# Value projections with tokens on partitions: 512 moving columns and four open PSUM banks in place of 256 columns and one

## The chip, the cores and the metric

The program runs on one core of a Trainium2 chip. The metric is device time in microseconds (us) of one execution, from the first to the last instruction; smaller is better. The kernel before has a median of 3309.61 us over three runs.

## The reference, cut to what matters

Two transformer blocks run one after the other on 512 tokens of 1024 channels, each with two layers. In the first block the normalised input h is multiplied by one wide matrix; the parts va and vb of the product are the values of two attention mixers:

```python
h = rmsnorm(x, norm1[l])
proj = h @ w_in[l]
qa, ka, va, qb, kb, vb, gate_pre = jnp.split(proj, splits, axis=-1)
o_a = dilated_mixture(hd4(qa, 12), hd4(ka, 12), hd4(va, 12))   # heads of 64, three groups of 4
o_b = stick_breaking_attention(hd4(qb, 4), hd4(kb, 4), hd4(vb, 4))
```

va has 768 columns (three head groups of 256), vb has 256. The second block does the same for two streams of tokens, 512 "latent" and 256 "context" tokens. Its mixer is a gated scan whose values are 512 columns of the input projection, plus a differential attention whose values are 256 columns, plus a Fourier part. Everything is float32; the kernel must come close to float32 results.

## The kernel before, in words

Activations lie with channels on partitions, as eight k tiles of 128 channels. To reach float32 accuracy each activation and each weight is kept as two parts, hi and lo, of a 32-bit format that TensorE multiplies in one pass, and each product is three matmuls: hi·hi, hi·lo, lo·hi.

Most projections (`proj_t`, with `mm3`, lines 131 to 142) take 128 weight columns as the stationary operand and 512 tokens as the moving one: 24 matmuls of 512 columns for one output tile. The value projections need tokens on partitions. `proj_n` (line 144) therefore takes 128 tokens of the activation as the stationary operand and 256 weight columns as the moving one: 24 matmuls of 256 columns for one block of 128 tokens, into one PSUM bank, of which they use half. Every matmul has its own weight load.

In the first block, `mixer1` (line 249) calls it for four chunks of 256 columns in each layer: vb right behind its queries and keys (lines 300 to 306); and behind the keys and queries of the other mixer three chunks, one for each head group of va (lines 313 to 320). The first of these takes blocks of 128 consecutive tokens. The other two take the tokens b, b + 4, b + 8, ...: the stationary operand is then read with a step of four elements,

```python
slice(b, T, 4) if c else slice(b * P, (b + 1) * P)
```

so 192 of the 384 value matmuls of a layer have stepped weight loads. Each block's result goes from PSUM to SBUF by one ScalarE instruction (line 306 or 320).

In the second block `natural` (line 760) does the same for the values of both streams (two chunks of 256 columns, called by `values`, line 858) and for the values of the differential attention (one chunk, called by `diff_in`, line 1159). Evacuations alternate between ScalarE (line 772) and VectorE (line 770). In the first layer the latent values stand behind the context's output projection and norm; in the second layer `weave` mixes them with the context's residual and norm steps, one step for each `yield`.

Weights come by `load_weights` (line 116) in pieces of 1024 columns on 128 partitions (512 KB): one DMA on SyncE's queue, a cast on ScalarE (hi, line 126), a subtraction on VectorE (lo, line 127). There are three buffers for raw, three for hi and two for lo. `weights` (line 106) gives the chunk that is wanted and asks for the next one; a chunk of 128 columns is one piece (all eight k tiles), a chunk of 256 columns is two pieces (four k tiles each).

PSUM in the mixer of the first block is cut into two "mm" banks, three "sc" banks for scores, two "at" and one "po"; in the second block's mixer into two "mm", two "lev", two "at" and a "ds" tile of two banks. Each engine works through its queue in order; the framework lays the queues out ahead of time, by the order of the program's text and by when operands are ready in its own planning.

Of the kernel before, what the change touches and what calls it, by code (L numbers as in the profile page):

```python
# [14 lines left out]
ALU = mybir.AluOpType  # L15
# [15 lines left out]
class Split:  # L31
    """A value kept as two float32r parts, each of [128, n]: hi + lo."""
# [8 lines left out]
class Stream:  # L41
    """Tokens that go through the second block: x tiles [128 channels, n]."""
# [5 lines left out]
class Net:  # L48
# [57 lines left out]
    def weights(self, src, kt, cols, ahead=True):  # L106
        """src: DRAM [128, kt, cols]; -> list over k of (hi, lo) slices. ahead: asks for the next ones, too."""
        self.asked.append((src.tensor.name, src.offset, [list(d) for d in src.ap], kt, cols))
        i = len(self.asked)
        out = self.ahead.pop() if self.ahead else self.load_weights(src, kt, cols)  # L110
        if ahead and i < len(self.plan):
            name, off, ap, kt, cols = self.plan[i]
            self.ahead.append(self.load_weights(bass.AP(self.io[name].tensor, off, ap), kt, cols))
        return out
# [22 lines left out]
    def proj_t(self, out, w, c0, xs, start=True, stop=True):  # L137
        """out[128 n, t] += W[:, c0:c0+128]^T x over the k tiles of xs."""
        for k, x in enumerate(xs):
            hi, lo = w[k]  # L140
            self.mm3(out, hi[:, c0:c0 + P], lo[:, c0:c0 + P], x.hi, x.lo,
                     start and k == 0, stop and k == len(xs) - 1)

    def proj_n(self, out, w, c0, n, xs, ts):
        """out[128 t, n] = x[:, ts]^T W[:, c0:c0+n]; ts: 128 tokens, a slice or the first one."""
# [9 lines left out]

    def split(self, dst, src, lo_src=None):
        """dst = src as two parts; src is float32 in SBUF or PSUM."""
# [14 lines left out]
    def rstd_cols(self, acc, nb, dim, classes=False):  # L172
        """acc [128, nb*128] of squares -> [128 t, nb] of 1/sqrt(mean + eps); column b is a block of tokens or,
        by classes, the tokens b, b + nb, ..."""
# [11 lines left out]
    def rstd_bcast(self, acc, nb, dim):  # L186
        """-> PSUM [128, nb*128]: 1/sqrt(mean + eps) of each token on every partition."""
# [14 lines left out]
    def gained(self, l, name, k):  # L202
        """x[k] * g as a split tile; the token's factor comes behind the product."""
# [7 lines left out]
    def token_factor(self, acc, classes=False):  # L211
        """1/rms of each token: on every partition, [128, t], and [128 t, block]; with classes also
        [128 i, r] of the tokens 4 i + r."""
# [7 lines left out]
    def scope(self, banks=None, **pools):  # L221
        """Opens pools for a part of the program; the exit stack closes them.
        banks: PSUM tag -> number of banks."""
# [25 lines left out]
    def mixer1(self, l, first):  # L249
# [24 lines left out]
        def proj_qk(c, n, scale):  # L274
            """-> [128 ch, t] tiles; those of the dilated groups, from the third of twelve heads' on, keep
            the tokens by classes: column 128 r + i is token 4 i + r."""
# [23 lines left out]
        w = self.weights(io["w_in_n"][l, 3], KT, 256)  # L300
        rh = self.small("rh", 4)
        nc.vector.tensor_scalar(rh, rcs[0], 0.5, None, ALU.mult)
        for b in range(4):
            ps = self.bank()
            self.proj_n(ps[:, :256], w, 0, 256, hs, b * P)
            nc.scalar.mul(vb[:, b, :], ps[:, :256], rh[:, b:b + 1])
        qa = proj_qk(0, 6, 0.125)
        ka = proj_qk(6, 6, 1.0)
# [4 lines left out]
        for i in range(3):  # L313
            w = self.weights(io["w_in_n"][l, i], KT, 256)
            c, j = min(i, 1), max(i - 1, 0)
            for b in range(4):
                ps = self.bank()
                self.proj_n(ps[:, :256], w, 0, 256, hs, slice(b, T, 4) if c else slice(b * P, (b + 1) * P))
                dst = va[c][b][:, 4 * j:4 * j + 4, 0:64]
                nc.scalar.mul(dst, ps[:, :256].rearrange("p (h d) -> p h d", h=4), rcs[c][:, b:b + 1])  # L320

        ob = [self.pv.tile([P, 256], F32, tag=f"ob{b}", name=self.nm("onat")) for b in range(4)]
        # sums of the dilated mixture by blocks (0) and classes (1) of tokens, with negated maxima and denominators
# [49 lines left out]
    def after(self, ins, before):  # L373
        """Keeps `ins` behind `before` in their engine's queue."""
# [58 lines left out]
    def weighted(self, out, blocks, width):  # L433
        """out[128 q, width] = sum over blocks of p^T-transposed @ v: blocks (p [128 q, 128 s], v [128 s, width])."""
# [14 lines left out]
    def dsw(self, s, qa, ka, va, sums, stat):  # L449
        """Head slot s of the three dilated groups: the first one's queries by blocks of 128 tokens, those of  # L450
        the other two, which see keys of their own class t % 4 alone, by classes and with one softmax."""
# [36 lines left out]
    def dsw_join(self, sums, stat):  # L488
        """The mixture over all three groups: sums times exp(max - joint max) / joint denominator. Each layout gets
        the other's maxima and denominators by way of memory. -> by layout, normalised [128 t, 256] tiles."""  # L490
# [27 lines left out]
    def stick(self, h, qb, kb, vb, on):  # L518
        """Head h of the stick-breaking mixer. With y = tanh(z / 2): sigmoid(z) = (1 + y) / 2 and
        1 - sigmoid(z) = (1 - y) / 2, whose product over the later keys is a scan from the right;  # L520
        the half of sigmoid is in vb."""
# [21 lines left out]
    def heads_t(self, on, name, classes=None):  # L543
        """[128 t, 256] of four blocks -> two split tiles [128 ch, t]; classes: a part to add, by classes."""
# [32 lines left out]
    def consts2(self):  # L577
# [12 lines left out]
        # forget gates f = mid + half * tanh(z / 2) and 1 - f = half - half * tanh(z / 2): [128, layer, dir * head]  # L590
# [19 lines left out]
    def lambdas(self):  # L610
        nc, io, pc = self.nc, self.io, self.pcx
        self.onorm, self.subln, self.neglam = [], [], []
        # the halves of the silus are in the values and in onorm
# [21 lines left out]
    def cond(self):  # L635
        """silu of both conditions, on every partition."""
# [11 lines left out]
    def modulation(self, l, before):  # L648
# [11 lines left out]
        for v in range(2):  # L660
            m = self.mods[l][v]
            nc.vector.tensor_tensor(m, m, self.v2("b_mod", 48 * l, 48), ALU.add)
            # 1 + scale times the norm's gain; gates times the gain behind them
# [10 lines left out]
    def adaln_steps(self, hs, st, m, sc, sh, alloc):  # L674
        """rms_norm(x) * gain * (1 + scale) + shift as split tiles."""
# [12 lines left out]
    def weave(self, first, *rest, rate=1.0):  # L688
        """Interleaves two chains of steps, rate of the second to one of the first; the second starts first."""
# [14 lines left out]
    def residual(self, st, acc, ys, m, gate, out=None, pe=False):  # L704
        """x += gate * rms_norm(y), in steps. out: the last one, which stores x. pe: TensorE sums the
        squares, for a norm that waits for them."""
# [25 lines left out]
    def pairs(self, pool, tag, name, n, bufs=None):  # L732
        """Allocator of split tiles of n tokens, packed into slots of 4 KB."""
# [26 lines left out]
    def natural(self, l, st, hs, first, out, scale=1.0):  # L760
        """Projection with tokens on partitions into the blocks out[b] [128, width]."""
        nc = self.nc
        for i in range(out[0].shape[1] // 256):
            w = self.weights(self.io["w_in2n"][l, first + i], KT, 256)
            for b, o in enumerate(out):
                ps = self.bank()
                self.proj_n(ps[:, :256], w, 0, 256, hs, b * P)
                dst = o[:, 256 * i:256 * (i + 1)]
                if b % 2:
                    nc.vector.tensor_scalar(dst, ps[:, :256], scale, None, ALU.mult)  # L770
                else:
                    nc.scalar.mul(dst, ps[:, :256], scale)
                yield

    def mixers2(self, l, st, sc, c, full):
        """Both streams' mixers. c: the context's input; full: the context goes on behind this layer.
        -> both streams' input of the feed forward."""
# [44 lines left out]
        else:  # L822
            # the second half's products lie behind the first half's norms; cat's tiles become the output
# [15 lines left out]
    def gpairs(self, name):  # L839
        """Allocator of the context's split tiles in the slots of the gates."""  # L840
# [17 lines left out]
    def values(self, l, st, hs, v):  # L858
        yield from self.natural(l, st, hs, 0, v, 0.5)

    def attend(self, l, st, hs, sc, v, side=iter(())):
        """The hgrn heads, the differential attention between their parts, the fourier input.
        side: steps that go along; the context's projections come first."""
# [32 lines left out]
    def mix_cat(self, l, st, a, alloc):  # L896
        """The mixer's output in front of the output projection."""
# [9 lines left out]
    def mix_out(self, l, st, cat, ys, acc, order=range(KT), kept=None):  # L907
        """The output projection of st's tokens, and its sum of squares. kept: weights by chunk, to which
        the last two are added."""
# [20 lines left out]
    def halves(self, st):  # L930
        """The stream's tokens in two parts, as (slice, stream)."""
# [10 lines left out]
    def gate(self, l, h, d, hs, n, t):  # L942
        """t = tanh(z / 2) of the forget gate, d: 0 forward, 1 backward."""
        self.nc.scalar.activation(t, self.proj2(l, 4 + 4 * d + h, hs, n), AF.Tanh, scale=0.5)

    def silu2(self, dst, ps, n):
        """2 * silu."""
# [4 lines left out]
    def state(self, st, h, kx, v):  # L952
        """Final states of the context: sum over tokens of key x value, keys kx [128 ch, (f, b), n]."""
# [14 lines left out]
    def states(self, l, st, h, hs, v):  # L968
        """The context's final states of a head, by products over the later or earlier gates."""
# [677 lines left out]
```

## Time and profile before

| | |
|---|---|
| runs, device time | 3307.6, 3309.61, 3320.05 us |
| median | 3309.61 us |
| profiled execution, span (the page has no other time of it) | 3308.6 us |
| TensorE matmul busy | 3250.8 us, 98% |
| TensorE weight loads busy | 2760.6 us, 83% |
| VectorE, ScalarE, GpSimd busy | 61%, 41%, 2% |
| DMA | 370.70 MB, mean 112 GB/s |
| mean granted TensorE clock | 0.993 of full speed |

A matmul's duration in the profile runs from its issue to its modelled end, so that neighbours overlap: matmuls of 512 columns start 0.23 us apart and last 0.39 us each. How fast TensorE goes is read from the starts (or from a count in a stretch), not from durations.

### The profile page before, as it was taken

The page shows a single profiled execution, that of the slowest core. Times are in us where ns is not written, and L with a number is a line of the kernel's source. Part 1 is how long each engine was busy: PE and PEld are TensorE (multiplying, and loading weights), DVE is VectorE, ACT ScalarE, POOL GpSimd, SP SyncE. Part 2 cuts the span into 40 slices and gives each one's busy share as a digit, 9 for nine tenths or more (in the row PEclk, how much of TensorE's full clock was granted, in tenths as well). Part 3 has the DMA queues.
Part 4 walks back from the last instruction along what each step waited for, and adds up shares of the span by engine and source line. Part 5 has one row for each costly group of instructions (what it writes and reads, how often), then busy time and mean ns, then how long its engine had stood idle before and what let it go on. Part 6 is the DMA issues. An engine that isn't in the chain of part 4 may idle for free. (4 is left out here: it accounts for less than half of the span.)

```text
span 3308.6 us, 48142 instructions
## 1 busy us (share of the span) xinstructions
PE 3250.8 (98%) x19480; PEld 2760.6 (83%) x19480; DVE 2006.8 (61%) x3318; ACT 1358.9 (41%) x2326; POOL 68.6 (2%) x213
## 2 busy tenths in 40 slices
PE   9999999999999999999999999999999999999998
PEld 7978888888978888889887789888899988888887
DVE  4265799753255799766867867333257677662335
ACT  3144432332144432346756755222235457542223
POOL 0000000000000000000100000000000100000000
PEclk9999999999999999999999999999999999999999
DMA  4213367533213366536342225333134522223333
GB/s 139 70 45 98 114 197 216 151 98 96 71 45 97 109 199 216 151 102 189 106 140 64 73 68 166 96 96 96 59 94 147 165 83 70 68 86 96 96 96 115
DMA packets 109231, 370.70 MB, mean 112 GB/s; under 512 B 13264, under 2 KB 18384, under 8 KB 109008
## 3 DMA queue, kind: packets, MB, share of 16 engines
q1 hardware_dynamic: 103824, 352.28, 35.0%
q0 software_dynamic: 5184, 15.34, 1.6%
q8 instruction: 153, 2.51, 0.3%
q14 instruction: 70, 0.57, 0.1%
HBM read 359.64 MB, written 7.93 MB: 111 GB/s over the span
## 5 line engine op out<-in xcount | busy, mean ns | idle before, releaser
L126 ACT CAST whi<-raw 128x1024 fp32r<-128x1024 f32 (+1 forms) x556 | 575.9, 1036 | 1137.9 <-PE mm L134 785.8
L127 DVE TENSOR_TENSOR wlo<-raw,whi 128x1024 fp32r<-128x1024 f32 (+1 forms) x556 | 667.0, 1200 | 383.8 <-PE mm L135 171.8
L133 PE MATMUL mm<-h,whi 128*128 128x512 f32 x1904 | 752.1, 395 | 11.9 <-ACT whi L126 6.7
L135 PE MATMUL mm<-h,wlo 128*128 128x512 f32 x1904 | 752.0, 395 | 0.0
L134 PE MATMUL mm<-h,whi 128*128 128x512 f32 x1904 | 750.5, 394 | 0.0
L133 PEld LDWEIGHTS mm<-h,whi 128*128 128x128 f32 x1904 | 358.4, 188 | 85.3 <-issue 8.4
L135 PEld LDWEIGHTS mm<-h,wlo 128*128 128x128 f32 x1904 | 358.1, 188 | 73.0 <-DVE wlo L127 1.7
L134 PEld LDWEIGHTS mm<-h,whi 128*128 128x128 f32 x1904 | 358.2, 188 | 72.7 <-issue 1.5
L135 PE MATMUL mm<-hid,wlo 128*128 128x512 f32 (+1 forms) x896 | 323.8, 362 | 3.2 <-DVE wlo L127 3.1
L133 PE MATMUL mm<-hid,whi 128*128 128x512 f32 (+1 forms) x896 | 324.1, 362 | 0.4 <-ACT whi L126 0.4
L134 PE MATMUL mm<-hid,whi 128*128 128x512 f32 (+1 forms) x896 | 324.3, 362 | 0.0
L135 PEld LDWEIGHTS mm<-hid,wlo 128*128 128x128 f32 x896 | 168.0, 188 | 31.4 <-DVE wlo L127 3.8
L134 PEld LDWEIGHTS mm<-hid,whi 128*128 128x128 f32 x896 | 168.2, 188 | 28.1 <-DVE hid L160 0.4
L133 PEld LDWEIGHTS mm<-hid,whi 128*128 128x128 f32 x896 | 168.1, 188 | 28.1 <-ACT whi L126 0.6
L133 PE MATMUL mm<-cat,whi 128*128 128x512 f32 (+1 forms) x512 | 186.4, 366 | 4.6 <-ACT cat L683 3.3
L135 PE MATMUL mm<-cat,wlo 128*128 128x512 f32 (+1 forms) x512 | 186.6, 365 | 0.0
L134 PE MATMUL mm<-cat,whi 128*128 128x512 f32 (+1 forms) x512 | 186.2, 365 | 0.0
L1376 DVE TENSOR_TENSOR silu<-silu,mm 128x512 f32<-128x512 f32 (+1 forms) x58 | 36.1, 623 | 222.9 <-PE mm L135 222.4
L153 PE MATMUL mm<-wlo,h 128*128 128x256 f32 x448 | 142.8, 319 | 0.5 <-DVE wlo L127 0.2
L152 PE MATMUL mm<-whi,h 128*128 128x256 f32 x448 | 141.5, 316 | 1.1 <-ACT y L752 1.1
L154 PE MATMUL mm<-whi,h 128*128 128x256 f32 x448 | 141.6, 316 | 0.0
L656 DVE SCALAR_TENSOR_TENSOR junk<-wmod,c 128x1024 f32<-128x1024 f32 x96 | 116.8, 1216 | 4.5 <-DMA wmod<-w_mod 4.1
(431 smaller groups left out, 5396.3 us busy)
## 6 DMA issues: line engine op xcount, KB each, us to landing
raw<-w_fi SPq DMA_DIRECT2D x120, 512.0 KB, 3.6
wmod<-w_mod SPq DMA_DIRECT2D x96, 512.0 KB, 4.3
raw<-w_up SPq DMA_DIRECT2D x88, 512.0 KB, 3.8
raw<-w_in2t SPq DMA_DIRECT2D x76, 512.0 KB, 3.6
raw<-w_in_t SPq DMA_DIRECT2D x64, 512.0 KB, 3.6
raw<-w_fo SPq DMA_DIRECT2D x48, 512.0 KB, 3.5
raw<-w_down SPq DMA_DIRECT2D x32, 512.0 KB, 3.6
raw<-w_out SPq DMA_DIRECT2D x28, 512.0 KB, 3.6
```

The lines of the kernel that those rows point to most:

```text
L126: nc.scalar.copy(hi, raw)
L127: nc.vector.tensor_tensor(lo, raw, hi.bitcast(F32), ALU.subtract)
L133: mm(out, lh, rh, start=start, stop=False)
L134: mm(out, lh, rl, start=False, stop=False)
L135: mm(out, ll, rh, start=False, stop=stop)
L152: mm(out, xh, hi[:, c0:c0 + n], start=k == 0, stop=False)
L153: mm(out, xh, lo[:, c0:c0 + n], start=False, stop=False)
L154: mm(out, xl, hi[:, c0:c0 + n], start=False, stop=k == last)
L656: ins = nc.vector.scalar_tensor_tensor(o, w, 1.0, cs[v], ALU.mult, ALU.mult, accum_out=self.mods[l][v][:, j:j + 1])
L1376: nc.vector.tensor_tensor(s, s, ps[1][:, :n], ALU.mult)
```

## The change

A new helper `wide` multiplies blocks of 128 tokens with 512 weight columns. It goes over the k tiles in four pairs; for each pair it asks for one piece of weights (two k tiles of 512 columns, again 1024 columns and 512 KB) and goes over all blocks, so that four PSUM banks (two "mm" and two "sc", or two "mm" and two "lev"; two "mm" for the context) stay open until the last pair. In the first block, one run of it makes vb and the first group of va from consecutive tokens, behind the queries and keys of the stick-breaking mixer; a second run makes the other two groups of va from the stepped tokens. Evacuations come behind the whole run: per consecutive block one ScalarE and one VectorE instruction of 256 columns, per stepped block one ScalarE instruction of 512. In the second block `natural` uses `wide` for the values of both streams; the differential attention's values stay at 256 columns. The weight arrays are laid out to match.

```diff
+    def wide(self, src, hs, blocks, banks):
+        out = []
+        last = KT - 1
+        mm = self.nc.tensor.matmul
+        for k0 in range(0, KT, 2):
+            w = self.weights(src[:, k0:k0 + 2, :], 2, 512)
+            for i, ts in enumerate(blocks):
+                if k0 == 0:
+                    out.append(self.bank(banks[i]))
+                for j, (hi, lo) in enumerate(w):
+                    k = k0 + j
+                    xh, xl = hs[k].hi[:, ts], hs[k].lo[:, ts]
+                    mm(out[i], xh, hi, start=k == 0, stop=False)
+                    mm(out[i], xh, lo, start=False, stop=False)
+                    mm(out[i], xl, hi, start=False, stop=k == last)
+                if i % 2:
+                    yield out
...
-        w = self.weights(io["w_in_n"][l, 3], KT, 256)
...
-        for b in range(4):
-            ps = self.bank()
-            self.proj_n(ps[:, :256], w, 0, 256, hs, b * P)
-            nc.scalar.mul(vb[:, b, :], ps[:, :256], rh[:, b:b + 1])
-        qa = proj_qk(0, 6, 0.125)
-        ka = proj_qk(6, 6, 1.0)
...
-        for i in range(3):
-            w = self.weights(io["w_in_n"][l, i], KT, 256)
-            c, j = min(i, 1), max(i - 1, 0)
-            for b in range(4):
-                ps = self.bank()
-                self.proj_n(ps[:, :256], w, 0, 256, hs, slice(b, T, 4) if c else slice(b * P, (b + 1) * P))
-                dst = va[c][b][:, 4 * j:4 * j + 4, 0:64]
-                nc.scalar.mul(dst, ps[:, :256].rearrange("p (h d) -> p h d", h=4), rcs[c][:, b:b + 1])
+        banks = ("mm", "mm", "sc", "sc")
+        heads = lambda a: a.rearrange("p (h d) -> p h d", d=64)
+        for ps in self.wide(io["w_in_n"][l, 0], hs, [slice(b * P, (b + 1) * P) for b in range(4)], banks):
+            pass
+        for b in range(4):
+            nc.scalar.mul(vb[:, b, :], ps[b][:, :256], rh[:, b:b + 1])
+            nc.vector.tensor_scalar(va[0][b][:, :, 0:64], heads(ps[b][:, 256:]), rcs[0][:, b:b + 1], None, ALU.mult)
+        qa = proj_qk(0, 6, 0.125)
+        ka = proj_qk(6, 6, 1.0)
+        for ps in self.wide(io["w_in_n"][l, 1], hs, [slice(b, T, 4) for b in range(4)], banks):
+            pass
+        for b in range(4):
+            nc.scalar.mul(va[1][b][:, :, 0:64], heads(ps[b]), rcs[1][:, b:b + 1])
...
+        if n == 512:
+            blocks = [slice(b * P, (b + 1) * P) for b in range(len(out))]
+            for ps in self.wide(self.io["w_in2v"][l], hs, blocks, ("mm", "mm", "lev", "lev")):
+                yield
             for b, o in enumerate(out):
...
+                put(b, o, ps[b])
+            return
...
-    m["w_in_n"] = st(lambda l: chunks(a["w_in"][l], KT, 256)[[6, 7, 8, 11]])
+    m["w_in_n"] = st(lambda l: chunks(a["w_in"][l][:, [*range(2816, 3072), *range(1536, 2304)]], KT, 512))
...
-    m["w_in2n"] = st(lambda l: chunks(a["w_in_2"][l], KT, 256)[[2, 3, 12]])
+    m["w_in2n"] = st(lambda l: chunks(a["w_in_2"][l], KT, 256)[12])
+    m["w_in2v"] = st(lambda l: chunks(a["w_in_2"][l][:, 512:1024], KT, 512)[0])
```

## Rows read from the trace of the kernel before

**Rows 1.** The page's head, part 1 and the clock line of part 2.
```profile
span 3308.6 us, 48142 instructions
PE 3250.8 (98%) x19480; PEld 2760.6 (83%) x19480; DVE 2006.8 (61%) x3318; ACT 1358.9 (41%) x2326; POOL 68.6 (2%) x213
...
PEclk9999999999999999999999999999999999999999
```

**Rows 2.** The page's costliest groups: a 512-column projection and the value matmuls.
```profile
L133 PE MATMUL mm<-h,whi 128*128 128x512 f32 x1904 | 752.1, 395 | 11.9 <-ACT whi L126 6.7
...
L153 PE MATMUL mm<-wlo,h 128*128 128x256 f32 x448 | 142.8, 319 | 0.5 <-DVE wlo L127 0.2
```

**Rows 3.** Stretches: us, busy (instructions) of PE, PEld, DVE, ACT, POOL; clock, DMA.
```profile
50.00:100.00 50.00, 50.00 (x222) 41.42 (x221) 18.11 (x18) 9.50 (x9) 0.00 (x0) 1.00 0.34 97
112.32:123.80 11.48, 11.48 (x97) 11.45 (x96) 3.42 (x3) 3.51 (x5) 0.00 (x0) 1.00 0.16 47
123.91:168.81 44.90, 44.90 (x195) 44.77 (x193) 4.98 (x5) 7.75 (x12) 0.00 (x0) 1.00 0.17 50
781.89:793.48 11.59, 11.59 (x97) 11.55 (x96) 3.05 (x3) 3.50 (x5) 0.00 (x0) 1.00 0.15 45
870.39:915.28 44.89, 44.89 (x195) 44.76 (x193) 4.98 (x5) 7.75 (x12) 0.00 (x0) 1.00 0.17 50
```

**Rows 4.** Timeline of weight loads, 80 us: the 512-column projection (start, duration).
```profile
79.91 0.19 PEld L135 LDWEIGHTS mm<-h,wlo 128*128 128x128 f32 x1
...
80.82 0.19 PEld L133 LDWEIGHTS mm<-h,whi 128*128 128x128 f32 x1
```

**Rows 5.** Timeline of weight loads at 123.8 us, where the stepped tokens begin.
```profile
123.44 0.19 PEld L152 LDWEIGHTS mm<-whi,h 128*128 128x128 f32 x1
123.56 0.19 PEld L153 LDWEIGHTS mm<-wlo,h 128*128 128x128 f32 x1
...
124.48 0.33 PEld L152 LDWEIGHTS mm<-whi,h 128*128 128x128 f32 x1
124.71 0.33 PEld L153 LDWEIGHTS mm<-wlo,h 128*128 128x128 f32 x1
```

**Rows 6.** Timelines of weight loads: one-column matmuls of line 179, consecutive, then stepped.
```profile
20.96 0.97 PEld L179 LDWEIGHTS ss<-cmat,acc 128*128 128x128 f32 x8 [0.26 <-DVE acc L170]
21.85 0.19 PEld L135 LDWEIGHTS sc<-h,wlo 128*128 128x128 f32 x1
...
24.14 1.95 PEld L179 LDWEIGHTS ss<-cmat,acc 128*128 128x128 f32 x8
25.99 0.21 PEld L133 LDWEIGHTS sc<-h,whi 128*128 128x128 f32 x1
```

**Rows 7.** Timelines of VectorE where a value run begins, in both layers.
```profile
112.58 1.23 DVE L127 TENSOR_TENSOR wlo<-raw,whi 128x1024 fp32r<-128x1024 f32 x1 [3.34 <-issue]
113.72 1.09 DVE L293 SCALAR_TENSOR_TENSOR qk<-mm,fac 128x512 f32<-128x512 f32 x1
...
783.29 0.69 DVE L290 SCALAR_TENSOR_TENSOR qk<-mm,fac 128x512 f32<-128x512 f32 x1
```

**Rows 8.** Stretches of the second block, columns as before: values twice, and a low clock.
```profile
1694.40:1720.41 26.01, 25.51 (x202) 24.52 (x203) 17.03 (x37) 12.22 (x22) 0.00 (x0) 1.00 0.26 81
...
2602.39:2624.37 21.98, 19.39 (x146) 18.84 (x145) 10.32 (x13) 8.31 (x12) 7.16 (x17) 0.92 0.85 261
1905.00:1930.00 25.00, 22.83 (x135) 19.66 (x136) 14.21 (x31) 14.79 (x44) 0.00 (x0) 0.84 0.11 32
```

**Rows 9.** Line 153: what TensorE sat idle for.
```profile
  DVE wlo L127: 5.3, 10
```

**Rows 10.** Line 320: its evacuations (duration in ns, minimum/median/maximum).
```profile
L320 ACT ACTIVATE va<-mm,r x24: 473/473/477, 115.5 to 915.4; 128x256 f32<-128x256 f32 x24
```

**Rows 11.** Timeline of TensorE where the attention of the first layer begins.
```profile
168.81 1.56 PE L527 MATMUL sc<-qk,qk 64*128 64x128 f32 x6
170.30 0.50 PE L133 MATMUL mm<-h,whi 128*128 128x512 f32 x1
```

More of the change, by code (lines that the diff above doesn't have):

```diff
@@ L299, in mixer1 @@
         kb = proj_qk(14, 2, 1.0)
-        w = self.weights(io["w_in_n"][l, 3], KT, 256)
-        rh = self.small("rh", 4)
-        nc.vector.tensor_scalar(rh, rcs[0], 0.5, None, ALU.mult)
-        for b in range(4):
-            ps = self.bank()
-            self.proj_n(ps[:, :256], w, 0, 256, hs, b * P)
-            nc.scalar.mul(vb[:, b, :], ps[:, :256], rh[:, b:b + 1])
-        qa = proj_qk(0, 6, 0.125)
-        ka = proj_qk(6, 6, 1.0)
         va = [[self.pv.tile([P, n, 65], F32, tag=f"va{c}{b}", name=self.nm("va")) for b in range(4)]
@@ L312, in mixer1 @@
             nc.gpsimd.memset(v[:, :, 64:65], 1.0)
-        for i in range(3):
-            w = self.weights(io["w_in_n"][l, i], KT, 256)
-            c, j = min(i, 1), max(i - 1, 0)
-            for b in range(4):
-                ps = self.bank()
-                self.proj_n(ps[:, :256], w, 0, 256, hs, slice(b, T, 4) if c else slice(b * P, (b + 1) * P))
-                dst = va[c][b][:, 4 * j:4 * j + 4, 0:64]
-                nc.scalar.mul(dst, ps[:, :256].rearrange("p (h d) -> p h d", h=4), rcs[c][:, b:b + 1])
+        rh = self.small("rh", 4)
+        nc.vector.tensor_scalar(rh, rcs[0], 0.5, None, ALU.mult)
+        banks = ("mm", "mm", "sc", "sc")
[11 more added lines that the diff above has]
+            nc.scalar.mul(va[1][b][:, :, 0:64], heads(ps[b]), rcs[1][:, b:b + 1])
         ob = [self.pv.tile([P, 256], F32, tag=f"ob{b}", name=self.nm("onat")) for b in range(4)]
@@ L758, in proj2, with natural @@
         return ps[:, :n]
-    def natural(self, l, st, hs, first, out, scale=1.0):
+    def natural(self, l, st, hs, out, scale=1.0):
         nc = self.nc
-        for i in range(out[0].shape[1] // 256):
-            w = self.weights(self.io["w_in2n"][l, first + i], KT, 256)
-            for b, o in enumerate(out):
[L766 to L773, printed above, removed]
+        n = out[0].shape[1]
+        put = lambda b, dst, ps: (nc.vector.tensor_scalar(dst, ps, scale, None, ALU.mult) if b % 2 else
+                                  nc.scalar.mul(dst, ps, scale))
+        if n == 512:
+            blocks = [slice(b * P, (b + 1) * P) for b in range(len(out))]
+            for ps in self.wide(self.io["w_in2v"][l], hs, blocks, ("mm", "mm", "lev", "lev")):
+                yield
+            for b, o in enumerate(out):
+                put(b, o, ps[b])
+            return
+        w = self.weights(self.io["w_in2n"][l], KT, 256)
+        for b, o in enumerate(out):
+            ps = self.bank()
+            self.proj_n(ps[:, :256], w, 0, 256, hs, b * P)
+            put(b, o, ps[:, :256])
+            yield
     def mixers2(self, l, st, sc, c, full):
@@ L858, in values @@
     def values(self, l, st, hs, v):
-        yield from self.natural(l, st, hs, 0, v, 0.5)
+        yield from self.natural(l, st, hs, v, 0.5)
     def attend(self, l, st, hs, sc, v, side=iter(())):
@@ L1158, in diff_in @@
             st.raws = raws
-        yield from self.natural(l, st, hs, 2, [st.dv[:, b, :] for b in range(nb)])
+        yield from self.natural(l, st, hs, [st.dv[:, b, :] for b in range(nb)])
     def rope(self, l, st):
```

## The prediction

> **What bounds the kernel now.** I read the page first: TensorE is busy for 98% of the span, no other engine for more than 61%, and the clock line shows nines in all 40 slices [rows 1]. So time that the change takes off TensorE's queue comes off the end, unless a wait appears. But busy time does not tell the pace. By the costliest groups a value matmul of 256 columns lasts 319 ns and one of 512 columns 395 ns [rows 2], which would make halving the count worth 243 ns for each pair. These durations overlap. I therefore went on to counts in stretches and to starts in the timeline.
>
> In the stretch from 50 to 100 us, 222 matmuls of 512 columns start in 50 us [rows 3]; in the timeline the first of five loads starts at 79.91 and the fifth at 80.82, four steps in 0.91 us [rows 4]: **0.227 us** each. The vb chunk of the second layer, from 781.89 us, has 96 matmuls of 256 columns in 11.59 us [rows 3]: **0.1207 us** each, so two of them cost 0.241 us. From consecutive tokens, then, 512 columns are only 14 ns cheaper than twice 256.
>
> The stretch from 123.91 to 168.81 us is different: 192 value matmuls of the same shape take 44.90 us [rows 3], **0.234 us** each, twice as long. The timeline shows the border: loads start 0.12 us apart and last 0.19 us up to 123.80, then they start 0.23 us apart and last 0.33 us [rows 5]. At that point the tokens change from consecutive ones to every fourth. The clock is 1.00 in both stretches, so it is not the clock.
>
> What sets 0.234? The one-column matmuls of line 179 answer it, since they have the same loads and next to nothing to stream. Eight with consecutive tokens go from 20.96 to 21.85 us, 0.111 us each; eight with stepped tokens from 24.14 to 25.99, 0.231 us each [rows 6]. A stepped load therefore costs 0.231 us with one column behind it and 0.234 us with 256 columns behind it: the load alone sets the pace and the columns stream beside the next load. Likewise 0.111 with one consecutive column and 0.1207 with 256.
>
> **The change part by part.** All pieces stay at 512 KB and 1024 columns, with the same number of DMAs, casts and subtractions; SyncE, and the casts, have the same work, so I cost them at nothing. What covers them: in the 44.90 us of the stepped stretch ScalarE has 7.75 us of work, VectorE 4.98, and DMA is at 0.17 [rows 3]. A run of four blocks uses up a piece in 24 x 0.23 = 5.5 us, as a 512-column projection does.
>
> (a) Stepped tokens, first block. Removed: 192 matmuls a layer, 44.90 and 44.89 us [rows 3]. Added: 96 of 512 columns with a stepped load each. The trace has no such pair. From below it cannot be faster than the stream, 0.227 [rows 4]; from above, load and stream in turn, 0.234 + 0.227 = 0.461. I take the load, 0.2335 (between 0.231 and 0.234), since the trace shows it unmoved by 256 columns of stream, and the stream of 0.227 still fits into it. 96 x 0.2335 = 22.4 us. Gain 22.5 a layer, **45.0 us** in two; by the bounds between 46.2 gained and 1.3 added.
>
> [...]
>
> (b) Consecutive tokens, first block. Removed: two chunks of 96 a layer, 11.59 us for vb and the stretch from 112.32 to where the stepped part starts at 123.91, 11.59 us [rows 3]. Added: 96 x 0.227 = 21.8. Gain 1.4 a layer, **2.8 us**.
>
> (c) Latent values, second block: 192 x 0.1207 = 23.2 becomes 96 x 0.227 = 21.8 in each layer: **2.8 us** in two. In the first layer they lie in a stretch where TensorE is busy for 25.51 of 26.01 us [rows 8]; the second layer's I take the same way.
>
> (d) Context values: 96 x 0.1207 = 11.6 becomes 48 x 0.227 = 10.9. In the second layer DMA is at 0.85 of its time and 261 GB/s and TensorE waits [rows 8], so there I count nothing, in the first layer **0.7 us**. Bounds 0 and 1.4.
>
> (e) A wait that is added. The second block of a run starts 6 matmuls after the first, not 24 x 0.12 = 2.9 us after it as now, and needs the other "mm" bank. VectorE empties that bank behind the lo subtraction of the next piece: behind the last keys, whose matmuls end their turn at 112.32 and in whose place the stepped run will follow, the subtraction starts at 112.58 and lasts 1.23, the evacuation of line 293 starts at 113.72 and lasts 1.09, so it ends at 114.81 [rows 7]. The new run would want the bank at 112.32 + 6 x 0.2335 = 113.72. TensorE waits 1.1 us, with the rest of the run behind it, in both layers. In the second layer's first run the evacuation of line 290 starts at 783.29 and lasts 0.69 [rows 7]; wanted 781.89 + 6 x 0.227 = 783.25: 0.7 us. In the first layer's first run the banks were emptied long before. Loss **2.9 us**; from below nothing, if the framework's planning of the queues puts the evacuation first. In the second block the same wait is an estimated 0.6 us in each of three runs (a start 0.26 us behind the matmuls and 1.23 for the subtraction as above [rows 7], 0.47 for an evacuation of 256 columns as on ScalarE [rows 10], less 1.36), but the 5.3 us that TensorE sat idle at line 153 for lo pieces [rows 9] shrink, since each piece is now wanted 5.5 us after the one before (2.7 us for the context) and never two at a chunk's border. I set these against each other: 0, bounds 3 gained and 2 lost.
>
> (f) Evacuations. Twelve of 0.47 us on ScalarE for va [rows 10] become four on VectorE and four longer ones. The last one, behind the stepped run, delays ScalarE ahead of the first tanh by some 0.2 us; TensorE is covered there by scores and by gate projections, which it starts 1.5 us into the attention [rows 11]. Cost 0; without that cover 0.2 us a layer.
>
> Sum: 45.0 + 2.8 + 2.8 + 0.7 - 2.9 = 48.4 us. From the profiled span, 3308.6, this gives 3260.2. The median of the runs shown lies 1.0 us above that span: **3261.2 us**, 1.5% faster.
>
> **The rivals.**
> *Load and stream in turn.* At 0.461 us a stepped matmul, term (a) is 2 x (96 x 0.461 - 44.9) = 1.3 us lost; with the other 3.4 gained the time is 3307.5. For it: the two would be nearly equally long, with little slack to hide in. Against it: 0.231 with one column, 0.234 with 256. Chance 5%. [...]
> *Half of the overlap lost.* With 512 columns streaming for nearly the whole load, reads disturb each other: 0.34 us each, (a) gains 24.5, time 3281.7. For it: no row has a stepped load beside more than 256 columns. Against it: the first 256 cost 3 ns. 5%.
> *The planner's order.* Both "mm" banks are held for 22 us, so that other projections of the second block's mixer can't stand among the latent values, and steps that had filled waits are missing elsewhere; the idle time in two such stretches is 0.5 and 2.6 us now [rows 8], and I price a bad order at 10: 3271. 3%.
> *Slower.* The stepped reads slow the stream as much as they slow the load, from 0.111 to 0.231: 512 columns at 0.45 in all are not enough for a loss, but 0.427 behind a load of 0.234 are 0.66 us; 96 x 0.66 = 63.4 against 44.9 a layer, 37 us lost, less 3.4: 3343. It decides from 0.485 us a matmul, where (a) loses the 3.4. The same two rows on 1 and 256 columns speak against it. 2%.
>
> **How the numbers follow.** The forecast has 85%. Within it the time can lie 4 to 8 us lower (no bank wait, lo waits gone) or 3 higher by the bounds above. TensorE's clock adds to both sides: around 1905 to 1930 us it is granted 0.84 [rows 8], 4 us lost, and where such stretches fall can change with the order; I allow 5. That is 3248 to 3270. To leave out no more than 2 in 10 the range goes on to the planner's and the half-lost overlap: 3247 to 3282. About 0.5% (16.5 us) is what a measurement of this kernel can tell from no change. The forecast, the half-lost overlap and the planner's order are all faster by more: 0.92 with a little off for what I did not think of. Load and stream in turn is the same, 0.05; slower 0.03.
>
> **What would show it.** Right: in the stepped run of the new kernel, loads of 0.33 us that start 0.23 us apart, 96 of them in 22 to 24 us, in both layers; the consecutive run at 0.227; one gap of about 1 us at the sixth matmul of a run, released by VectorE. Wrong: stepped starts 0.3 us or more apart (then the overlap was a matter of slack), a first-block mixer that is 45 us shorter while the second block's is longer (the planner), or new low-clock stretches.

## The result and the profile after

| | before | after |
|---|---|---|
| median of the runs that were timed together (4 each) | 3311.11 us | 3259.95 us |
| lowest and highest | 3307.6 to 3320.05 | 3258.58 to 3261.87 |
| span of the profiled execution | 3308.6 us | 3258.1 us |

The ratio is 0.9844, with a 95% interval of 0.9828 to 0.986: the changed kernel is 1.6% faster, some 51 us. The forecast was 3261.2 us, with a range of 3247 to 3282.

The page of the changed kernel, with its head, part 1 and the clock line of part 2 (the columns are those of [rows 1]):

```profile
span 3258.1 us, 46766 instructions
PE 3196.9 (98%) x18808; PEld 2684.9 (82%) x18808; DVE 2009.5 (62%) x3320; ACT 1353.8 (42%) x2304; POOL 68.7 (2%) x213
...
PEclk9999999999999999999999999999999999999999
```

672 matmuls are gone, TensorE is busy for 53.9 us less, and its share of the span is still 98%. The span has shrunk by 50.5 us. No other engine moved by more than 6 us. So TensorE bounded the kernel and does so still; nearly all of its saved time went off the end.

Where it went is seen in stretches of the changed kernel: the consecutive and the stepped run of the first layer, the same two of the second layer, and part of the latent values in the second block's first layer. The columns are length, busy time (instructions) of PE, PEld, DVE, ACT and POOL, granted clock, DMA share and GB/s:

```profile
34.80:56.56 21.76, 21.76 (x97) 18.02 (x96) 6.98 (x9) 5.65 (x7) 0.00 (x0) 1.00 0.32 98
121.85:144.71 22.86, 22.86 (x98) 22.49 (x97) 5.93 (x6) 6.24 (x7) 0.00 (x0) 1.00 0.30 92
758.52:780.28 21.76, 21.76 (x97) 18.02 (x96) 6.97 (x9) 5.62 (x7) 0.00 (x0) 1.00 0.34 98
845.56:868.55 22.99, 22.99 (x97) 22.63 (x96) 5.91 (x6) 6.27 (x7) 0.00 (x0) 1.00 0.30 92
1654.86:1673.57 18.71, 18.71 (x85) 15.49 (x84) 12.98 (x27) 7.61 (x13) 0.00 (x0) 1.00 0.26 86
```

The stepped tokens took 44.90 and 44.89 us [rows 3] and now take 22.86 and 22.99: 43.9 us of the 50.5 lie here. The consecutive tokens took twice 11.59 us a layer and now take 21.76: 2.8 us in two layers. What is left is 3.8 us.

Weight loads in the middle of the changed kernel's stepped run (start, duration), to be set beside [rows 5]:

```profile
132.87 0.31 PEld L172 LDWEIGHTS sc<-whi,h 128*128 128x128 f32 x1
133.10 0.31 PEld L170 LDWEIGHTS mm<-whi,h 128*128 128x128 f32 x1
133.34 0.31 PEld L171 LDWEIGHTS mm<-wlo,h 128*128 128x128 f32 x1
133.57 0.31 PEld L172 LDWEIGHTS mm<-whi,h 128*128 128x128 f32 x1
133.81 0.31 PEld L170 LDWEIGHTS mm<-whi,h 128*128 128x128 f32 x1
```

Four steps in 0.94 us: a stepped load still starts every 0.235 us, though twice as many columns now stream beside it.

The wait that was foreseen at the second block of a run, in the changed kernel's timeline of TensorE (the first layer's stepped run, which begins at 121.85):

```profile
122.78 0.40 PE L171 MATMUL mm<-wlo,h 128*128 128x512 f32 x1
123.03 0.39 PE L172 MATMUL mm<-whi,h 128*128 128x512 f32 x1
123.25 0.61 PE L170 MATMUL mm<-whi,h 128*128 128x512 f32 x1
123.69 0.40 PE L171 MATMUL mm<-wlo,h 128*128 128x512 f32 x1
```

and of VectorE (the evacuation of the last keys, then the lo subtraction):

```profile
122.05 1.13 DVE L313 SCALAR_TENSOR_TENSOR qk<-mm,fac 128x512 f32<-128x512 f32 x1 [3.28 <-PE mm L135]
123.02 1.21 DVE L127 TENSOR_TENSOR wlo<-raw,whi 128x1024 fp32r<-128x1024 f32 x1
```

There is one step of 0.44 us at the seventh matmul, 0.2 us longer than its neighbours. In [rows 7] the subtraction stood first and the evacuation second; now it is the other way round, and the bank is empty a microsecond earlier than forecast.

### The profile page after: what moved, and what is told of

Read it like the earlier page. It is cut to its first block, busy times and chain, and to the rows that moved or that the text cites. A ratio compares the mean times of both kernels' runs of the same rounds, so it can differ in the third digit from the quotient of the medians.

```text
span 3258.1 us, 46766 instructions
## 1 busy us (share of the span) xinstructions
PE 3196.9 (98%) x18808; PEld 2684.9 (82%) x18808; DVE 2009.5 (62%) x3320; ACT 1353.8 (42%) x2304; POOL 68.7 (2%) x213
## 4 chain that ended last, share of the span: by engine, by line
PE 91%; DVE 3%; ACT 3%; DMA 2%; issue 1%; SPq 0%; DVEq 0%; ACTq 0%
PE mm L133 24%; PE mm L135 24%; PE mm L134 24%; PE at L1258 2%; PE sc L478 1%; PE po L500 1%; PE ds L1236 1%; DVE wlo L127 1%; PE mm L170 1%; PE mm L171 1%; PE mm L172 1%; DMA raw<-w_in2v 1%; ACT whi L126 1%; PE sc L545 1%; PE at L1254 1%
## 5 line engine op out<-in xcount | busy, mean ns | idle before, releaser
L674 DVE SCALAR_TENSOR_TENSOR wmod<-wmod,c 128x1024 f32<-128x1024 f32 x96 | 116.8, 1217 | 0.7
L133 PEld LDWEIGHTS mm<-cat,whi 128*128 128x128 f32 x512 | 97.4, 191 | 20.5 <-ACT cat L701 3.6
L134 PEld LDWEIGHTS mm<-cat,whi 128*128 128x128 f32 x512 | 97.2, 190 | 15.1
```

The lines of the kernel that those rows point to most:

```text
L133: mm(out, lh, rh, start=start, stop=False)
L134: mm(out, lh, rl, start=False, stop=False)
L674: ins = nc.vector.scalar_tensor_tensor(o, w, 1.0, cs[v], ALU.mult, ALU.mult, accum_out=self.mods[l][v][:, j:j + 1])
```

## The experiments

The theory to be tested: a weight load from every fourth token takes 0.234 us whatever streams behind it, and the gain is the number of such loads that went away. The rival: each matmul (or instruction) that goes away saves the same, 51.2 us / 672 = 0.076 us. The first four kernels ran on one chip beside 13 runs of the kernel before (median 3309.34 us).

**e1: the stepped run alone at 512 columns.**

```diff
-        for i in range(3):
+        w = self.weights(io["w_in_n"][l, 0], KT, 256)
...
+        for ps in self.wide(io["w_in_w"][l], hs, [slice(b, T, 4) for b in range(4)], ("mm", "mm", "sc", "sc")):
+            pass
```

> Only the stepped tokens' run is made 512 columns wide; all other value projections stay at 256. Theory (the stepped weight load sets the pace, 0.234 us a matmul, whatever streams behind it): 192 matmuls a layer of 0.234 us become 96 of 0.238, 22.0 us less a layer, 44 us in all, about 3267 us against 3311. Rival (every matmul that goes away saves the same share of the whole gain, 51.2 us / 672 = 0.076 us): 192 matmuls less, 14.6 us, about 3296.5.

Measured: 3267.14 us, ratio 0.9874 [0.9859, 0.9889], 42 us less. Its stepped runs, in the two layers (columns as above):

```profile
126.70:149.44 22.74, 22.74 (x98) 22.50 (x96) 4.97 (x5) 6.64 (x8) 0.00 (x0) 1.00 0.38 115
851.40:874.21 22.81, 22.81 (x98) 22.57 (x97) 4.97 (x5) 6.64 (x8) 0.00 (x0) 1.00 0.37 116
```

Some 22.8 us as in the full change. The time is the theory's, and 29 us away from the rival's: 192 of the 672 matmuls carry 42 of the 51 us.

**e2: all but the stepped run.**

```diff
-        for ps in self.wide(io["w_in_n"][l, 1], hs, [slice(b, T, 4) for b in range(4)], banks):
-            pass
+        for i in range(2):
+            w = self.weights(io["w_in_s"][l, i], KT, 256)
...
+                self.proj_n(ps[:, :256], w, 0, 256, hs, slice(b, T, 4))
```

> The change, with the stepped tokens' run put back to two chunks of 256 columns. Theory: what is left is the difference of 14 ns between one matmul of 512 and two of 256 columns, 480 times, 6.7 us, less or more by waits: 3303 to 3306 us against 3311. Rival (every matmul less saves the same): 480 x 0.076 = 36.6 us less, about 3274.5.

Measured: 3308.19 us over 10 runs, ratio 0.9995 [0.9984, 1.0005]: between 5 us faster and 2 us slower. The 6.7 us that the theory expected lie outside that, so this expectation missed; the rival's 36.6 us are excluded by far more. The profiled execution, which is the fastest of the ten, has a span of 3302.7 us, 5.9 less than before; 4.3 of these lie in a place where the kernel before had a clock of 0.85 and this one has 1.00 (terms (c), (d) below). Its runs from consecutive tokens and from stepped ones:

```profile
35.46:57.22 21.76, 21.76 (x97) 18.02 (x96) 6.98 (x9) 5.64 (x7) 0.00 (x0) 1.00 0.32 98
122.50:167.28 44.78, 44.78 (x193) 44.65 (x192) 5.96 (x6) 7.38 (x11) 0.00 (x0) 1.00 0.13 38
```

21.76 as in the full change, 44.78 as before. Four open banks and half the matmuls, without the stepped loads, are worth little.

**e3: the kernel before, without the step.** Consecutive tokens in all chunks, so two head groups of va hold the wrong tokens; no matmul and no column less.

```diff
-                self.proj_n(ps[:, :256], w, 0, 256, hs, slice(b, T, 4) if c else slice(b * P, (b + 1) * P))
+                self.proj_n(ps[:, :256], w, 0, 256, hs, slice(b * P, (b + 1) * P))
```

> The kernel before, with consecutive tokens also where it takes every fourth (so two head groups of va hold the wrong tokens); the number of matmuls and columns is unchanged. Theory: 384 matmuls go from 0.234 to 0.1207 us, 43.5 us less, about 3267.5 against 3311. Rival (the gain is one of instructions or columns): no change, 3311.

Measured: 3265.44 us, ratio 0.9875 [0.9859, 0.9892], 44 us less. The 192 matmuls of each layer that had been stepped:

```profile
124.50:147.69 23.19, 23.19 (x194) 23.06 (x193) 4.90 (x4) 7.77 (x12) 0.00 (x0) 1.00 0.29 91
849.30:872.37 23.07, 23.07 (x193) 22.94 (x192) 4.90 (x4) 7.76 (x12) 0.00 (x0) 1.00 0.30 92
```

0.120 us each in place of 0.234 [rows 3]. So the step is the cause, shown without touching the width.

**e4: the changed kernel, without the step** (the same wrong tokens).

```diff
-        for ps in self.wide(io["w_in_n"][l, 1], hs, [slice(b, T, 4) for b in range(4)], banks):
+        for ps in self.wide(io["w_in_n"][l, 1], hs, [slice(b * P, (b + 1) * P) for b in range(4)], banks):
```

> The changed kernel, with consecutive tokens also in its second run (two head groups of va hold the wrong tokens). Theory: 192 matmuls go from 0.238 to 0.227 us, 2.1 us less than the change, about 3258 against 3311 for the kernel before; the second run takes 21.8 us in place of 22.9. Rival that load and stream still disturb each other at 512 columns: a larger gain than that, from whatever part of 0.238 is not the load's own 0.234.

Measured: 3257.15 us, ratio 0.9848 [0.9833, 0.9863]. Against the changed kernel this can't be told from no difference, as expected. Its second runs:

```profile
122.51:144.50 21.99, 21.99 (x97) 17.75 (x95) 5.90 (x6) 6.27 (x7) 0.00 (x0) 1.00 0.33 96
845.67:867.65 21.98, 21.98 (x97) 17.76 (x95) 5.89 (x6) 6.26 (x7) 0.00 (x0) 1.00 0.32 97
```

21.99 against 22.86 us and 21.98 against 22.99: all that is left of the step behind 512 columns is 1.9 us in two layers. A version that gets rid of it would win about that much here, too little for the times to show; none was built.

**e5: steps of two and three** in the kernel before (chunk 2 of va with every second token, chunk 3 with every third; wrong tokens).

```diff
-                self.proj_n(ps[:, :256], w, 0, 256, hs, slice(b, T, 4) if c else slice(b * P, (b + 1) * P))
+                self.proj_n(ps[:, :256], w, 0, 256, hs, (slice(b * P, (b + 1) * P), slice(b // 2 * 256 + b % 2, b // 2 * 256 + b % 2 + 255, 2), slice(b, b + 382, 3))[i])
```

> The kernel before, its second chunk of va with every second token and its third chunk with every third (wrong tokens, same counts). What makes the stepped load slow? [...] If it grows with the step: step 2 at 0.15, step 3 at 0.19. If any step at all does it: both at 0.234.

Measured in one execution: 3282.68 us, against 3315.49 for the kernel before on the same chip. The stretches of 96 matmuls each, step two, then step three (the second layer has the same lengths):

```profile
126.63:138.14 11.51, 11.51 (x98) 11.51 (x97) 2.45 (x2) 3.91 (x6) 0.00 (x0) 1.00 0.29 91
138.15:155.11 16.96, 16.96 (x98) 16.84 (x96) 2.46 (x3) 3.88 (x6) 0.00 (x0) 1.00 0.20 63
```

A step of two costs nothing (0.120 us a matmul), a step of three gives 0.177 us. Even growth from step one on (0.15 and 0.19) and a price on any step (0.234 twice) are out. Reckoned from the 0.2335 us at step four in proportion to the step, step three would take 0.175 us and step two 0.117, which hides under the 0.120 of the stream. That is an estimate, and it fits both; at step one it does not hold, where eight loads with one column behind each take 0.111 us each [rows 6] and not 0.058. Steps above four were not tried, and what in the load makes it so is not shown by any run.

**e6: two pieces of weights at once** in the changed kernel.

```diff
-            w = self.weights(src[:, k0:k0 + 2, :], 2, 512)
+            if k0 % 4 == 0:
+                both = self.weights(src[:, k0:k0 + 4, :], 4, 512)
+            w = both[k0 % 4:k0 % 4 + 2]
```

> The changed kernel, with two pieces of weights asked for at once (so that two are asked for ahead, as the chunks of 256 columns did). Theory: the order of the text then puts the lo subtraction of the next piece ahead of the last evacuation of the keys in VectorE's queue, and the second block of the stepped run waits about 1.1 us for its bank in place of 0.2, the first run of the second layer 0.7 us in place of none; 2 to 3 us more in all. Rival (the framework planned the evacuation first for its own reasons): order and gaps as in the changed kernel, 0.2 us.

Measured in one execution: 3260.23 us, span 3258.4. VectorE's timeline at the start of the stepped run, which begins at 122.02:

```profile
122.28 1.22 DVE L127 TENSOR_TENSOR wlo<-raw,whi 128x1024 fp32r<-128x1024 f32 x1 [3.34 <-issue]
123.42 1.07 DVE L315 SCALAR_TENSOR_TENSOR qk<-mm,fac 128x512 f32<-128x512 f32 x1
```

and TensorE's:

```profile
123.67 0.40 PE L173 MATMUL sc<-wlo,h 128*128 128x512 f32 x1
123.90 0.40 PE L174 MATMUL sc<-whi,h 128*128 128x512 f32 x1
124.64 0.60 PE L172 MATMUL mm<-whi,h 128*128 128x512 f32 x1 [0.34 <-DVE qk L315]
125.08 0.39 PE L173 MATMUL mm<-wlo,h 128*128 128x512 f32 x1
```

The order of [rows 7] is back, and with it the wait for VectorE: steps of 0.74 and 0.44 us, 0.7 us more than two plain ones, against 0.2 in the changed kernel. It is less than the 1.1 expected; the framework moved three matmuls of the third block (into an "sc" bank) ahead of the second block, which fill a part of it. The other sizes missed as well: the first run of the second layer takes 21.99 us in place of 21.76, 0.2 us more where 0.7 were expected, and the span is 0.3 us longer than the changed kernel's and not 2 to 3. The order of VectorE's queue follows from how many pieces are asked for ahead; the change halved that, by its pieces of two k tiles.

**e7: 384 and 448 columns behind the stepped load** (first and second layer; the missing heads get copies of others).

```diff
-                    mm(out[i], xh, hi, start=k == 0, stop=False)
+                    mm(out[i][:, :n], xh, hi[:, :n], start=k == 0, stop=False)
...
+        for ps in self.wide(io["w_in_n"][l, 1], hs, [slice(b, T, 4) for b in range(4)], banks, (384, 448)[l]):
```

> The changed kernel, whose second (stepped) run streams only the first 384 columns in the first layer and 448 in the second (the missing heads get copies of others). What are the 4 ns by which 0.238 us with 512 columns stands over 0.2335 with 256? If stream and load disturb each other in proportion to the columns: 0.2355 at 384 and 0.2365 at 448. If it comes only when the stream (0.227 us at 512 columns) is nearly as long as the load: 0.2335 in both.

Measured in one execution: 3266.74 us. The part behind the bank wait, 89 loads each (first layer 384 columns, second layer 448):

```profile
123.50:144.32 20.82, 20.82 (x90) 20.64 (x89) 4.28 (x5) 5.67 (x9) 0.00 (x0) 1.00 0.36 102
848.90:870.06 21.16, 21.16 (x90) 20.95 (x89) 4.23 (x5) 5.68 (x9) 0.00 (x0) 1.00 0.33 100
```

From start to start that is 0.2335 us with 384 columns and 0.238 with 448. With 512 the changed kernel has 0.235 in its first layer and 0.2366 in its second, and e1, e6 and e8 have 0.235 in both. The 0.238 that the expectations name for 512 columns is not the mean, since in the first layer steps of 0.232 to 0.233 us alternate with steps of 0.237 to 0.238. The 384 columns speak against a disturbance in proportion to the columns; the other expectation, no loss before the stream is nearly as long as the load, holds at 384 and fails at 448. Each width stands in one layer of one execution, and 512 columns by themselves differ by 1.6 ns between runs without a known cause, so what sets these last nanoseconds stays open. They are worth 0.4 us a run at most (96 x 4 ns).

**e8: the "sc" banks first.**

```diff
-        banks = ("mm", "mm", "sc", "sc")
+        banks = ("sc", "sc", "mm", "mm")
```

> The changed kernel with the first block's runs opening the two sc banks first and the mm banks for their third and fourth blocks. Theory (the gap of 0.2 us at the second block is the wait for the mm bank that VectorE empties): the gap is gone in both stepped runs, 0.4 us in all. Rival: the wait only moves, since the queries behind the first run, or the gate projections behind the second, now want mm banks that are emptied last; a gap of up to 1 us behind the runs.

Measured in one execution: 3262.2 us, span 3260.4. Its two stepped runs:

```profile
124.37:147.02 22.65, 22.65 (x97) 1.00 0.32 94
847.16:869.81 22.65, 22.65 (x97) 1.00 0.30 94
```

(TensorE alone: length, busy time, clock, DMA share, GB/s.) 22.65 against 22.86 and 22.99: the bank wait is gone, 0.4 of the 0.5 us in two layers. No step over 0.25 us stands at the end of the first runs, and behind the stepped runs TensorE stays busy although the first gate projection comes 1.5 us into the attention in place of 0.85, so the wait did not move. That the whole is not shorter is the start: this execution's first run begins at 37.28 us in place of 34.80, behind a stretch from 25 to 38 us whose granted clock is 0.87. It is no part of the edit: e1 and e5 have the same stretch.

## Why the prediction was right

*What bounds it.* TensorE's queue: 53.9 us of busy time less, 50.5 us of span less.

*(a) Stepped tokens, 45.0 us.* Right, and for the reason given. 96 x 0.2335 = 22.4 us was forecast for a run; without its bank wait it takes 22.65 (e8), 0.235 us a matmul. Gain 43.9 us with the wait, 44.5 without. That a load with one column and a load with 256 took nearly the same time in the trace of before (0.231 and 0.234 us, [rows 3, 6]) was the evidence that decided, and e3 shows the cause by itself: taking the step away gains 44 us at 256 columns, and 1.9 us at 512 (e4). The step's price did not vanish; it went under the longer stream (0.227 us of the 0.235).

*Load and stream in turn.* At 0.461 us a stepped matmul the run would have been 44 us long. It is 22.9. The rivals with half the overlap lost (0.34 us) and with a slowed stream (0.66) fall by the same row.

Two of the prediction's prices are wrong; the forecast does not use them. Load and stream in turn would have cost 96 x 0.461 = 44.3 us a layer, less than the 44.9 removed: 1.3 us gained and not lost, so that rival's time is 3304.9 us and not 3307.5 (the bound of term (a) has the same wrong sign). And a stream slowed as much as the load is 0.227 x 0.231 / 0.111 = 0.472 us; no row gives the 0.427 that the slower rival uses.

*(b) Consecutive tokens, 2.8 us.* 2 x (23.18 - 21.76) = 2.8.

*(c), (d) Second block, 3.5 us.* 3.8 us of the span are left beside (a) and (b), but this agreement is luck: by the stretches below they come from the clock, and all the rest together gave nothing. The latent values do run at the forecast pace: 82 of them one after the other in 18.71 us, 0.228 each. The context's values and those of its differential attention, in the second layer, got worse. The first row below is this place in the changed kernel, the second its counterpart of the low clock around 1905 us [rows 8]:

```profile
2551.68:2574.82 23.14, 18.57 (x98) 14.60 (x97) 11.66 (x14) 8.58 (x12) 8.21 (x18) 1.00 0.87 265
...
1854.00:1879.00 25.00, 21.13 (x143) 17.44 (x142) 16.23 (x34) 16.16 (x48) 0.00 (x0) 1.00 0.07 22
```

23.14 us against 21.98 [rows 8], at 0.87 of DMA's time: if the data sets the pace there, fewer matmuls save nothing, as term (d) assumed, and 1.2 us were lost on top. The stretch of low clock (0.84, [rows 8]) has no counterpart 51 us earlier (second row). What that gave is seen between the same two points of the program, the last transpose of one head's output and the first of the next, before and after:

```profile
1881.60:1927.30 45.70, 41.12 (x383) 33.59 (x381) 32.21 (x67) 27.43 (x71) 0.00 (x0) 0.85 0.12 36
...
1834.40:1875.80 41.40, 36.85 (x382) 29.41 (x380) 31.70 (x67) 26.81 (x70) 0.00 (x0) 1.00 0.13 39
```

The same work takes 4.3 us less at a granted clock of 1.00 than at one of 0.85. Up to 1834.40 us the changed kernel is 47.2 us ahead, of which (a) and (b) are 46.7; behind 1875.80 it loses 1.0 us. So everything outside (a), (b) and this place together loses 0.5 us, where 3.5 us were forecast for the second block's values, and the clock gave 4.3. Shorter stretches of low clock lie elsewhere in both traces (0.86 from 2875 to 2900 us in the changed kernel, from 1650 to 1675 in before); they were not separated from the rest. The change may well have a part in the full clock of this place: before, e1 and e3, whose second block is as before, have 0.85, 0.92 and 0.92 there; the changed kernel, e2, e4, e6 and e8 have 1.00. Why is open.

*(e) The added wait, 2.9 us lost.* This term was mis-sized: it is 0.2 us in each stepped run and nothing in the second layer's first run, 0.4 us in all. The step that failed is the order on VectorE. The forecast took it from [rows 7], where the lo subtraction stands ahead of the evacuation, and gave the other order only as its lower bound. The order there was itself a product of what the change removes: a chunk of two pieces asked for ahead puts the second piece's subtraction ahead of the evacuation in the program's text. e6 brings two pieces back, and with them that order and a wait of 0.7 us.

*(f) Evacuations, 0.* The last evacuation of the stepped run grew from 0.47 to 0.69 us; the attention's first score still comes right behind the run:

```profile
144.38 0.40 PE L172 MATMUL sc<-whi,h 128*128 128x512 f32 x1
144.71 0.92 PE L545 MATMUL sc<-qk,qk 64*128 64x128 f32 x4
145.56 0.50 PE L133 MATMUL mm<-h,whi 128*128 128x512 f32 x1
```

Gate projections fill in from 145.56 on, as in [rows 11].

*The total* was forecast at 48.4 us and came to 50.5 by the profiled spans: 2.5 us more by the bank wait, some 0.6 less by the stepped runs' pace, 4.3 more by the clock and 4.0 less by all the rest, where the second block's values stood with 3.5. The mechanism of the 45.0 us is shown; that the rest adds up to within 2 us is luck.

How much of the whole goes with the clock, the other runs show. In the 13 runs of the kernel before that stood beside e1 to e4, the span goes with the mean granted clock, from 3314.6 us at 0.992 to 3301.3 at 0.996. The changed kernel's four runs have 0.994 to 0.997. At 0.994 the two kernels are 45 to 48 us apart (3304.8 to 3307.5 against 3260.0), at 0.996 they are 43 us apart (3301.3 against 3258.1). So some 4 to 8 of the measured 51 us go with the clock. The 42 us of e1 and the 1 us of e2 also add up to 43 and not to 51.

## What to carry to other kernels

Measure a matmul's pace from start to start, by operand layout: the same shape ran at 0.12 and at 0.234 us here, and a mean over the line hid it. Where a stationary operand is read with a step of four 32-bit words, as here, put as many columns behind each load as a bank holds (512 here, at 0.235 to 0.2366 us a load against 0.234 with 256), or arrange the data so that the step is two or one (0.120 us with 256 columns, e5 and e3). And where a change alters how far ahead weights are asked for, work out the queue order anew from the program's text; the old trace shows the old order. Before a difference of two spans is shared out among terms, compare the granted clock of the two stretch by stretch.

## What the runs showed of the hardware that was not expected

- Loads of 128 columns from 32-bit words: 0.111 us or less at step one (one column behind it [rows 6]), hidden under 0.120 at step two, 0.177 at step three, 0.2335 at step four (e5, [rows 3]).
- A stepped load's pace is 0.2335 us with 256 and with 384 columns behind it, 0.238 with 448 and 0.235 to 0.2366 with 512 (e7, e8 and the changed kernel); the differences above 384 are unexplained.
- The first value run of otherwise equal starts begins between 34.6 (e7) and 38.2 us (e1). In e1, e5 and e8, which are late, the clock granted from 25 to 38 us is 0.87, in the other seven traces it is 1.00.
- The same work in the second block's first layer takes 41.40 us at a granted clock of 1.00 (the changed kernel, e2, e4, e6, e8; between the points of (c), (d)), 43.5 and 43.7 us at 0.92 (e3, e1) and 45.70 us at 0.85 (before).
